# Operands of an output projection made in an earlier stage and kept in DRAM, its last two token tiles by plain products, and GpSimd's sums there on DVE

## Chip, cores, metric

The kernel runs on one core of a Trainium2 chip. The metric is the device time of one launch in microseconds, median over runs. A core has five engines that run their own instruction queues in order: TensorE (PE in the profile, its weight loads PEld), VectorE (DVE), ScalarE (ACT), GpSimd (POOL) and SyncE (SP), which here issues nearly all transfers. SBUF is the memory on the chip, PSUM the accumulators of the matmuls, DRAM the memory off it.

## The reference

One layer of a bidirectional encoder for two sequences, 1024 and 256 tokens of width D = 1024, together T = 1280 tokens, all in float32.

```
h = rms_norm(x, norm_g) * (1 + scale) + shift
p = h @ w_in                       # gates, the conv branch, q, k, v, o, z
y_conv = cb * conv3(cc * cx) * silu(cz)
y_m    = sigmoid(o) * norm(mlstm both ways(q, k, v, gates)) * silu(mz)
merged = g_conv * (y_conv @ w_proj_conv) + g_mlstm * (y_m @ w_proj_mlstm)
return rms_norm(x + gate * (merged @ w_out), final_norm_g)
```

The change concerns w_out (1024 x 1024, the output projection) and the last two lines.

## The kernel before, in words

Float32 accuracy is had from faster matmuls: each operand is split into a high part (a cast on ACT, "wh" or "H") and a low part (source minus high part, "wl" or "L"), and each matmul becomes three: high x high, high x low, low x high. Large products are done by Strassen's scheme: a 2 x 2 block product takes seven products of sums of blocks, where the plain way takes eight of the blocks themselves.

The work stands in this order.

1. The main stage, the input projection (L809). One product is 24 matmuls of 128 x 320: 4 slices k, 3 part pairs, 2 token groups. For each, `prep` loads raw weights (512 KB a pair), DVE makes a sum where the scheme asks for one (L674), ACT casts (L319) and POOL subtracts (L320). Each wh and each wl lies in one of four slots of a ring; a slot comes free when the last instruction that reads it is done. The first 77 products are the gate part with the first head's products; then `gate_inputs` runs, and `advance(n)` emits products up to number n.
2. The mLSTM stage, with further matmuls woven in (L1403 to L1652).
3. The merging stage (`merge`, L1855 to L1857): 16 blocks, each of two products of 24 matmuls of 128 x 320, one for each branch and token half. Results of two units share a PSUM tile of two banks; DVE reads each (L619) and multiplies it by a gate. Loads named th and zc bring gates and earlier results from DRAM. In blocks 4, 6, 9 and 11, `prepare(k)` makes a quarter of the operands of the output projection out of w_out: four loads of 256 KB, sums on DVE (L1800), splits on ACT (L1776) and DVE (L1778), eight stores of 256 KB. Operands b11, b21 and t2 stay in SBUF; t1, t3, t4 and b22 go to DRAM (L1797) and are fetched later.
4. The output stage: tokens in two quads (512 tokens each) and a pair (256). Each takes seven Strassen products (L1947 to L1949) of matmuls 512 columns wide. A product's results go from PSUM through DVE (L1974), get the gate (L1988), are added to x (L1992), squared and summed on ACT (L1997), and normed (L2040, L2036). POOL does a few of these: sums of the next tokens' blocks (L1921), multiplications by the norm's gain (`weigh`, L2122) and, for the pair, one gate and one addition. Of the pair, the very last product is done in two halves of 256 columns, with a short chain behind each (L2230 to L2237), then square root, Newton step and scaling (L2241 to L2266), and the stores of the output.

A class `Board` collects the instructions of a stage with their buffers, and plays them in an order that a cost model finds; each carries a step, and a later step may not go far ahead of an earlier one. The order on each engine is fixed at the build, and a wait holds everything behind it on the same engine.

Of the kernel before, what the change touches and what calls it, by code (L numbers as in the profile page):

```python
# [181 lines left out]
def encoder_kernel(  # L182
# [41 lines left out]
    late_dr = {nm: dram.tile([2, P, 4, 512], F32, name=nm + "_dr") for nm in ("t1", "t3", "t4", "b22")}  # L224
# [1049 lines left out]

    beginning()
    advance(ends[0] - 10)
# [475 lines left out]
    prstack = ctx.enter_context(ExitStack())  # L1752
    pr = prstack.enter_context(tc.tile_pool(name="pr", bufs=7))
# [28 lines left out]
    def prepare(k):  # L1782

        r11, r12, r21, r22 = raws = [buf(pr, [P, 512], F32, "pr", 7) for _ in range(4)]
        for i, raw in enumerate(raws):
            kt, n0 = k + 4 * (i // 2), 512 * (i % 2)
            load(256, lambda raw=raw: raw[:], w_out[0, kt * P:(kt + 1) * P, n0:n0 + 512], (), [raw], True)

        def kept_split(dst, x):
            split_into(lambda: dst[:, 0, k], lambda: dst[:, 1, k], lambda: x[:], [x], (dst, 0, k), (dst, 1, k))  # L1790

        def away(nm, x, spent=True):
            h = buf(pr, [P, 512], F32R, "pr", 7)
            l = x if spent else buf(pr, [P, 512], F32R, "pr", 7)
            split_into(lambda: h[:], lambda: l[:].bitcast(F32R), lambda: x[:], [x], h, l)
            for i, t in enumerate((h, l)):
                op("SP", 256, lambda i=i, t=t: dma(late_dr[nm][i, :, k], fp(t[:])), r=[t], w=[(nm, i, k)], low=True)  # L1797

        def comb(out, x, y, o=ALU.subtract):
            op("DVE", .69, lambda: V.tensor_tensor(out=out[:], in0=x[:], in1=y[:], op=o), r=[x, y], w=[out])  # L1800

        kept_split(B11, r11)
        kept_split(B21, r21)
        away("b22", r22, False)
        comb(r22, r22, r12)
        comb(r12, r12, r11)
        comb(r11, r22, r11, ALU.add)
        away("t1", r12)
        away("t3", r22)
        kept_split(T2, r11)  # L1810
        comb(r21, r21, r11)
        away("t4", r21)
# [65 lines left out]
    class Tokens:  # L1878
# [60 lines left out]
        def product(self, nm, rhs, dst, cs=slice(0, 512)):  # L1939

            for j in range(self.n):
                ap, tok = dst[j]
                wh, wl = self.ws[nm][j]
                for k in range(4):
                    def mm(k=k, ap=ap, wh=wh, wl=wl):
                        m = ap()[:, 0:cs.stop - cs.start]
                        PE.matmul(m, wh[:, k], rhs[:, 0, k, cs], start=k == 0, stop=False)  # L1947
                        PE.matmul(m, wh[:, k], rhs[:, 1, k, cs], start=False, stop=False)  # L1948
                        PE.matmul(m, wl[:, k], rhs[:, 0, k, cs], start=False, stop=k == 3)  # L1949
                    op("PE", .72 * (cs.stop - cs.start) / 512, mm, r=[wh, wl, (rhs, 0, k), (rhs, 1, k)] + ([tok] if k else []), w=[tok])  # L1950
# [127 lines left out]
    prstack.close()  # L2078
# [6 lines left out]
    def fetch(nm):  # L2085
        b = buf(late, [P, 2, 4, 512], F32R, "late", 3)
        for i in range(2):
            for k in (0, 2):
                load(512, lambda i=i, k=k: fp(b[:, i, k:k + 2]), late_dr[nm][i, :, k:k + 2], (), [(b, i, k), (b, i, k + 1)])
        return b  # L2090
# [35 lines left out]
    for st, nxt in ((quad0, quad1), (quad1, pair)):  # L2126
# [15 lines left out]
        if st is quad1:  # L2142
            weigh(0, 0)
# [7 lines left out]
        do(st, "s1", t1, d)  # L2151
        w = st.plus(u3, d, o_tile("o"))
# [7 lines left out]
        if st is quad1:  # L2160
            t3 = fetch("t3")
# [4 lines left out]
        nxt.sums(True)  # L2166
# [7 lines left out]
        if st is quad1:  # L2174
            weigh(0, 1)
# [4 lines left out]
    banks_ = [buf(pool, [P, 2, 512], F32, "acc", 1 if pool is psD else 3) for pool in (psO, psO, psO, psD)]  # L2180
    b, d, c, a, f, e, *gb = [[((lambda t=t, i=i: t[:, i]), (t, i))] for t in banks_ for i in range(2)]

    def out(eng, ap, half, toks, c):
# [3 lines left out]
        else:  # L2187
            op("SP", 256, lambda: dma(q, ap()), r=toks)

    do(st, "a11", B11, b)  # L2190
    s1 = st.copy_out(b, "raw")
    parts(st, "s1", "s2")
    do(st, "s1", t1, d)
    t4 = fetch("t4")
    parts(st, "a12")
    do(st, "s2", T2, c)
    st.rest()
    u2 = st.plus(s1, c, o_tile("o"))
    u4 = st.plus(u2, d, o_tile("raw"))
    st.gated(0, 1, u4, square=False, pool=True)  # L2200
    parts(st, "s3")
    do(st, "a12", B21, a)
    st.plus(s1, a)
    st.gated(0, 0, s1)
    weigh(0, 0)
    parts(st, "s4")
    do(st, "s3", t3, f)
    u3 = st.plus(u2, f, o_tile("raw"))
    w = st.plus(u3, d, o_tile("o"))
    st.gated(1, 1, w)  # L2210
    weigh(1, 1)
    st.gated(1, 0, u3, square=False)
    parts(st, "a22")
    do(st, "s4", b22, e)
    t = o_tile("o")
    st.gated(0, 1, t, e)
    weigh(0, 1)
    ms, q_, t_ = (buf(small, [P, 1], F32, "l" + nm, 1) for nm in "mqt")
    ssq, ssq0 = st.ssq[1], st.ssq[0]
    op("DVE", .1, lambda: V.tensor_scalar(out=ms[:], in0=ssq[:, 0, 1:2], scalar1=1.0 / D, scalar2=EPS, op0=ALU.mult,  # L2220
                                          op1=ALU.add), r=[(ssq, 0, 1)], w=[ms])
    lt = o_tile("raw")
    oap, otoks = st.out_place(1, 0)
    hap, htoks = st.out_place(1, 1)
    gate0 = st.gate(1, 0)
    for i in range(2):
        do(st, "a22", t4, gb[i], cs=slice(256 * i, 256 * i + 256))
# [36 lines left out]
    for half in range(2):  # L2264
        ap, toks = st.out_place(0, half)
        op("ACT", .57, lambda ap=ap: A.activation(ap(), ap(), AF.Copy, bias=0.0, scale=q[:, 0:1]), r=[q, *toks], w=toks)  # L2266
        out("SP", ap, half, toks, 7)
# [30 lines left out]
```

## Time and profile before

| | us |
|---|---|
| median of three runs (1681.29 to 1687.9) | 1683.1 |
| the profiled execution, timed | 1685.18 |
| its span from first to last instruction | 1683.1 |
| merging stage | 1437.3 to 1563.9 |
| quads | 1563.9 to 1644.1 |
| pair, PE's part | 1644.1 to 1668.4 |
| behind the last matmul | 1668.4 to 1683.1 |

Rows of the profile give busy time, count and mean; rows of the timeline give start and length in us, engine, line and operation, and in brackets how long the engine had been idle and what released it.

### The profile page before, as it was taken

Reading aid. Unit: us, or ns where it says so; the run is one execution under the profiler, and the core shown is the slowest. Engines: PE = TensorE matmul, PEld = TensorE weight load, DVE = VectorE, ACT = ScalarE, POOL = GpSimd, SP = SyncE. Lnnn points to the kernel's source line nnn. Section 1 sums busy time; section 2 is a strip of 40 time slices with the busy share of each in tenths; the row PEclk is TensorE's granted clock in tenths of the full one; section 3 lists DMA queues with packets and bytes.
Section 4 is the critical chain, followed back from the end, with each engine's and each line's share of the span. In section 5 each row is a group of like instructions: output and inputs, shape, how many; then the busy total and the mean of one; then the engine's idle time right before and its main releaser. Section 6 shows DMA issues by size and latency. Waiting matters only on the chain.

```text
span 1683.1 us, 27858 instructions
## 1 busy us (share of the span) xinstructions
PE 1626.4 (97%) x10480; PEld 1555.1 (92%) x10480; DVE 1050.0 (62%) x1764; ACT 588.1 (35%) x1145; POOL 678.2 (40%) x492
## 2 busy tenths in 40 slices
PE   6999999999999999999999999999999999989995
PEld 3989999999999999999999999999988898989774
DVE  5785433556555656556666887551267777657798
ACT  4643331135443222222222212212256665423243
POOL 1343333335564666666766533333210002333112
PEclk8999999999999999999999999999999999999998
DMA  9434335324552122222222556459778855888854
GB/s 361 128 100 134 101 105 116 85 64 135 154 153 92 50 73 70 70 82 71 67 60 87 145 130 141 120 124 318 241 244 291 264 159 174 286 301 283 293 176 174
DMA packets 293929, 261.80 MB, mean 156 GB/s; under 512 B 97588, under 2 KB 239140, under 8 KB 293796
## 3 DMA queue, kind: packets, MB, share of 16 engines
q1 hardware_dynamic: 293492, 259.76, 50.2%
q8 instruction: 83, 1.36, 0.3%
q14 instruction: 50, 0.41, 0.1%
q10 hardware_dynamic: 304, 0.27, 0.1%
HBM read 182.70 MB, written 77.28 MB: 154 GB/s over the span
## 4 chain that ended last, share of the span: by engine, by line
PE 86%; DVE 5%; DMA 5%; issue 1%; SPq 1%; ACT 1%; POOL 0%; ACTq 0%; DVEq 0%; POOLq 0%
PE acc L809 64%; PE u L1443 3%; PE qc L1403 3%; PE acc L1650 2%; PE acc L1651 2%; PE acc L1652 2%; PE acc L1947 2%; PE acc L1948 2%; PE acc L1949 2%; DMA th<-th_dr 1%; PE misc L1526 1%; PE misc L1486 1%; SPq L308 1%; DMA raw<-in_w_proj_mlstm_dram 1%; DMA raw<-in_w_in_dram 1%
## 5 line engine op out<-in xcount | busy, mean ns | idle before, releaser
L320 POOL TENSOR_TENSOR wl<-comb,wh 128x512 fp32r<-128x512 f32 x176 | 249.7, 1419 | 288.2 <-ACT wh L319 283.9
L320 POOL TENSOR_TENSOR wl<-raw,wh 128x512 fp32r<-128x512 f32 x168 | 236.4, 1409 | 306.3 <-ACT wh L319 279.9
L718 DVE TENSOR_TENSOR q<-acc,q 128x640 f32<-128x640 f32 x272 | 220.8, 819 | 220.5 <-PE acc L809 215.2
L809 PE MATMUL acc<-xt,wh 128*128 128x320 f32 x1408 | 263.9, 309 | 0.0
L809 PEld LDWEIGHTS acc<-xt,wh 128*128 128x128 f32 x1408 | 220.8, 188 | 0.2
L319 ACT CAST wh<-raw 128x512 fp32r<-128x512 f32 x168 | 103.6, 620 | 323.4 <-PE acc L809 210.4
L319 ACT CAST wh<-comb 128x512 fp32r<-128x512 f32 x176 | 108.8, 619 | 296.2 <-PE acc L809 259.5
L809 PE MATMUL acc<-xt,wl 128*128 128x320 f32 x704 | 160.4, 309 | 0.0
L1609 POOL TENSOR_TENSOR wl<-raw,wh 128x512 fp32r<-128x512 f32 x28 | 36.6, 1310 | 223.3 <-ACT wh L1608 216.2
L809 PEld LDWEIGHTS acc<-xt,wl 128*128 128x128 f32 x704 | 117.7, 188 | 0.0
L674 DVE TENSOR_TENSOR comb<-raw 128x512 f32<-128x512 f32 x88 | 71.6, 814 | 45.1 <-DMA raw<-in_w_in_dram 32.6
L877 POOL TENSOR_TENSOR big<-big,q 128x640 f32<-128x640 f32 x48 | 78.6, 1638 | 37.3 <-DVE q L718 28.9
L616 ACT ACTIVATE q<-q,zero 128x640 f32<-128x640 f32 x76 | 63.1, 831 | 83.7 <-DVE q L718 78.1
L674 DVE TENSOR_TENSOR comb<-raw,comb 128x512 f32<-128x512 f32 x44 | 46.6, 1060 | 62.9 <-POOL wl L320 62.9
L809 PE MATMUL acc<-t3L,wh 128*128 128x320 f32 x352 | 81.5, 313 | 2.7 <-DVE t3L L371 2.7
L809 PE MATMUL acc<-t3H,wh 128*128 128x320 f32 x352 | 81.2, 312 | 1.4 <-ACT t3H L370 1.4
L809 PE MATMUL acc<-b00H,wh 128*128 128x320 f32 x352 | 82.4, 316 | 0.0
L809 PE MATMUL acc<-b10H,wh 128*128 128x320 f32 x352 | 80.7, 310 | 0.8 <-ACT q L732 0.8
L809 PE MATMUL acc<-t3H,wl 128*128 128x320 f32 x352 | 81.3, 312 | 0.0
L809 PE MATMUL acc<-b11H,wh 128*128 128x320 f32 x352 | 81.1, 312 | 0.0
L809 PE MATMUL acc<-b00L,wh 128*128 128x320 f32 x352 | 80.8, 311 | 0.0
L809 PE MATMUL acc<-t2L,wh 128*128 128x320 f32 x352 | 80.4, 310 | 0.1
(400 smaller groups left out, 4096.5 us busy)
## 6 DMA issues: line engine op xcount, KB each, us to landing
raw<-in_w_in_dram SPq DMA_DIRECT2D x120, 256.0 KB
raw<-in_w_in_dram SPq DMA_DIRECT2D x34, 512.0 KB
late<-t_dr SPq DMA_DIRECT2D x24, 512.0 KB
th<-th_dr SPq DMA_DIRECT2D x31, 320.0 KB
th_dr<-q SPq DMA_DIRECT2D x28, 320.0 KB
raw<-in_w_proj_conv_dram SPq DMA_DIRECT2D x16, 512.0 KB
raw<-in_w_proj_mlstm_dram SPq DMA_DIRECT2D x16, 512.0 KB
k<-kn_dr SPq DMA_DIRECT2D x56, 128.0 KB
```

The costliest lines, as they stand in the source:

```text
L319: op("ACT", .63, lambda: A.copy(wh[:], src()), r=r, w=[wh])
L320: op("POOL", 1.4, lambda: G.tensor_tensor(out=wl[:], in0=src(), in1=fp(wh[:]), op=ALU.subtract), r=[*r, wh], w=[wl])
L616: A.activation(out, in_, AF.Tanh, bias=zero[:, 0:1], scale=0.5)
L674: op("DVE", .9, lambda: V.tensor_tensor(out=t[:], in0=x(), in1=y(), op=o), r=[x.tok, y.tok], w=[t])
L718: op("DVE", .82, lambda: V.tensor_tensor(out=two(dst()), in0=acc[:, :, 0:TQ], in1=two(t()), op=ALU.add), r=[acc, t.tok], w=[dst.tok])
L809: PE.matmul(acc[:, q, 0:TQ], st_[:, k_, :], m_[:, q * TQ:(q + 1) * TQ], start=k_ == 0 and n == 0, stop=k_ == 3 and n == 2)
L877: op("POOL", 1.65, lambda: G.tensor_tensor(out=dst(), in0=dst(), in1=t(), op=ALU.mult), r=[dst.tok, t.tok], w=[dst.tok])
L1403: PE.matmul(pq[:, 0:HD + 2], qTs[i][:, kd, c * P:(c + 1) * P], C[:, kd, :], start=kd == 0, stop=kd == 1)
L1443: PE.matmul(pu[:, db, 0:HD + 2], k[:, db * P:(db + 1) * P], wv[:], start=True, stop=True)
L1609: op("POOL", 1.36, lambda wh=wh, wl=wl, src=src: G.tensor_tensor(out=wl[:], in0=src(), in1=fp(wh[:]), op=ALU.subtract), r=[raw, wh], w=[wl])
L1650: PE.matmul(acc[:, :TQ], wh, yH, start=kt == 0, stop=False)
L1651: PE.matmul(acc[:, :TQ], wh, yL, start=False, stop=False)
```

## The change

There are four edits.

The splits of w_out move from the merging stage to the main stage. A generator `out_weights` runs beside the products 31 to 70: for each of four k it loads four blocks of 256 KB, and then, one operand with each product, makes eight operands: cast on ACT (L1293), subtraction on POOL (L1294), in wh and wl slots of the same ring of four, and two stores of 256 KB (L1297) to DRAM; four sums go to DVE (L1300). That is 32 casts, 32 subtractions, 64 stores, 16 sums and 16 loads. The merging stage now only fetches b11, b21 and t2, 12 loads of 512 KB.

The generator yields 40 times, so that product 70 is emitted in its loop; `advance(ends[0] - 7)` then sets the counter back to 70, and `advance(ends[0])` emits product 70 again: 24 more matmuls of 128 x 320, one more POOL subtraction and two more raw loads of 512 KB.

The pair is done by plain products: eight in place of seven, of the four blocks of tokens without sums, each pair of products summed in PSUM; the last two of them are done in halves of 256 columns (48 matmuls in place of 24). Operand b12 is fetched for it, t3 and t4 only for the quads.

On POOL, the sums of the second quad go to DVE, the pair's sums and the pair's gate and addition are gone, and so are four multiplications of the second quad, which are now in DVE's scaling. Two multiplications stay on POOL for the pair, and one half of the last tile is scaled on DVE in place of ACT.

```diff
+    def out_weights():
+        for k in range(4):
+            places = [big() for _ in range(2)]
...
+            for _ in range(1 + 4 * (k == 0)):
+                yield
+            def parts(nm, x):
+                wh, wl = (buf(wp, [P, 4, P], F32R, t, 4) for t in ("wh", "wl"))
...
+                op("ACT", .63, lambda: A.copy(flat(wh), x[0]()), r=[x[1]], w=[wh])
+                op("POOL", 1.4, lambda: G.tensor_tensor(out=flat(wl), in0=x[0](), in1=fp(flat(wh)), op=ALU.subtract),
+                   r=[x[1], wh], w=[wl])
+                for i, t in enumerate((wh, wl)):
+                    op("SP", 256, lambda i=i, t=t, k=k: dma(op_dr[nm][i, :, k], fp(flat(t))), r=[t], low=True)
...
+            yield parts("b22", r22)
+            yield parts("b12", r12)
+            comb(r22, r22, r12)
+            yield parts("t3", r22)
...
     beginning()
-    advance(ends[0] - 10)
+    advance(31)
+    for _ in out_weights():
+        advance(at[0] + 1)
+    advance(ends[0] - 7)
     board.step = at[0]
     gate_inputs()
     advance(ends[0])
...
-        if i in (4, 6, 9, 11):
-            prepare((4, 6, 9, 11).index(i))
+        if i in (5, 7, 9):
+            n_ = (5, 7, 9).index(i)
+            fetch_into((B11, B21, T2)[n_], ("b11", "b21", "t2")[n_], low=True)
...
-        nxt.sums(True)
+        if nxt is quad1:
+            nxt.sums()
...
+    left, right = ("a11", "a12"), ("a21", "a22")
+    parts(st, "a12", "a21", "a22")
+    both_halves(0, left, (B11, B21), p0)
+    st.gated(0, 0, o_tile("raw"), p0)
     weigh(0, 0)
...
     for i in range(2):
-        do(st, "a22", t4, gb[i], cs=slice(256 * i, 256 * i + 256))
+        both_halves(1, right, (b12, b22), gb[i], cs=slice(256 * i, 256 * i + 256))
```

What this does to the order shows on POOL in the gate part of the main stage. Before, ahead of the first head's products, POOL's queue is one subtraction for each product (L320; comb and raw are sums and raw weights):

```order
L320 TENSOR_TENSOR wl_2485<-comb_2265,wh_2476 128x512 [waits DVE_49,PE_49,Activation_49]
L320 TENSOR_TENSOR wl_2519<-comb_2300,wh_2511 128x512 [waits DVE_49,PE_49,Activation_49]
L320 TENSOR_TENSOR wl_2560<-comb_2232,wh_2552 128x512 [waits PE_49,Activation_49]
L320 TENSOR_TENSOR wl_2587<-raw_2196,wh_2577 128x512 [waits PE_49,Activation_49]
L320 TENSOR_TENSOR wl_2626<-comb_2333,wh_2615 128x512 [waits DVE_49,PE_49,Activation_49]
```

At the end of the same part now, w_out's subtractions (L1294, from big) alternate with those of the products (L320):

```order
L320 TENSOR_TENSOR wl_2944<-raw_2631,wh_2924 128x512 [waits PE_49,Activation_49]
L1294 TENSOR_TENSOR wl_2960<-big_2811,wh_2947 128x512 [waits PE_49,Activation_49,Pool_49]
L320 TENSOR_TENSOR wl_3007<-comb_2717,wh_2996 128x512 [waits PE_49,Activation_49,Pool_49]
L1294 TENSOR_TENSOR wl_3016<-big_2691,wh_2999 128x512 [waits DMAHW2_49,DMAHW0_49,Activation_49]
L320 TENSOR_TENSOR wl_3037<-comb_2760,wh_3027 128x512 [waits PE_49,Activation_49]
L1294 TENSOR_TENSOR wl_3051<-big_2811,wh_3039 128x512 [waits PE_49,Activation_49]
L320 TENSOR_TENSOR wl_3074<-comb_2674,wh_3059 128x512 [waits DMAHW0_49,Activation_49]
L1294 TENSOR_TENSOR wl_3092<-big_2691,wh_3071 128x512 [waits DMAHW3_49,PE_49,Activation_49]
L320 TENSOR_TENSOR wl_3120<-raw_2631,wh_3108 128x512 [waits DMAHW0_49,Activation_49]
L1294 TENSOR_TENSOR wl_3132<-big_2691,wh_3112 128x512 [waits DMAHW2_49,Activation_49]
L320 TENSOR_TENSOR wl_3153<-comb_2796,wh_3124 128x512 [waits PE_49,Activation_49]
L1294 TENSOR_TENSOR wl_3173<-big_2691,wh_3151 128x512 [waits PE_49,Activation_49]
```

Ahead of each of a product's subtractions there now stands one of w_out's, and both wait for PE or for a store where their slot was last used. In the addresses that the build gives, the slots before go round strictly in four; now wl_2944, wl_3007, wl_3037 and wl_3051 lie in one and the same slot, one after the other, and wl_3120, wl_3153 and wl_3173 in another.

SP's queue in the merging stage before has stores of the operands (L1797) among the loads that the stage itself needs (zc, th):

```order
L1797 DMA b22_dr_80<-pr_15654 128x512 [waits DMAHW2_49,Activation_49]
L1797 DMA b22_dr_80<-pr_15664 128x512 [waits DMAHW3_49,DVE_49]
L1797 DMA t1_dr_77<-pr_15694 128x512 [waits DMAHW4_49,Activation_49]
L1797 DMA t1_dr_77<-pr_15560 128x512 [waits DMAHW5_49,DVE_49]
L1797 DMA t3_dr_78<-pr_15716 128x512 [waits DMAHW6_49,Activation_49]
L308 DMA zc_15736<-zc_dr_64 128x640 [waits DMAHW7_49,DVE_49]
L308 DMA th_15738<-th_dr_72 128x640 [waits DMAHW0_49]
```

Now the same queue, some blocks into the stage, has whole loads of made operands (t2) in their place, with waits on transfers only:

```order
L308 DMA t2_15764<-t2_dr_79 128x1024
L308 DMA t2_15764<-t2_dr_79 128x1024 [waits DMAHW3_49]
L308 DMA zc_15784<-zc_dr_64 128x640 [waits DMAHW4_49,DVE_49]
L308 DMA th_15793<-th_dr_72 128x640 [waits DMAHW6_49,DMAHW5_49]
L308 DMA zc_15814<-zc_dr_64 128x640 [waits DVE_49]
L308 DMA th_15817<-th_dr_72 128x640 [waits DMAHW7_49]
```

The loads of the stage thus no longer stand behind stores that wait for casts and subtractions.

More of the change, by code (lines that the diff above doesn't have):

```diff
@@ L1780, in split_into, with fetch_into @@
             op("POOL", 1.4, lambda: G.tensor_tensor(out=lo(), in0=src(), in1=fp(hi()), op=ALU.subtract), r=[*r, wh], w=[wl])
[L1782 to L1812, printed above, removed]
+    def fetch_into(b, nm, ks=(0, 2), low=False):
+        for i in range(2):
+            for k in ks:
+                load(512, lambda i=i, k=k: fp(b[:, i, k:k + 2]), op_dr[nm][i, :, k:k + 2], (), [(b, i, k), (b, i, k + 1)], low)
     def second_ym(n):
@@ L1937, in rest, with product @@
             self.comb(self.places[0, 1], self.places[0, 1], self.places[0, 0])
[L1939 removed]
+        def product(self, nm, rhs, dst, cs=slice(0, 512), start=True, stop=True):
             for j in range(self.n):
@@ L2086, in fetch @@
         b = buf(late, [P, 2, 4, 512], F32R, "late", 3)
-        for i in range(2):
-            for k in (0, 2):
-                load(512, lambda i=i, k=k: fp(b[:, i, k:k + 2]), late_dr[nm][i, :, k:k + 2], (), [(b, i, k), (b, i, k + 1)])
+        fetch_into(b, nm)
         return b
@@ L2188, in out, with both_halves @@
             op("SP", 256, lambda: dma(q, ap()), r=toks)
[L2190 to L2204, printed above, removed]
-    weigh(0, 0)
[L2206 to L2217, printed above, removed]
+    def both_halves(r, lhs, rhs, dst, **kw):
+        for i in range(2):
+            do(st, lhs[i], rhs[i], dst, start=i == 0, stop=i == 1, **kw)
+    left, right = ("a11", "a12"), ("a21", "a22")
+    parts(st, "a12", "a21", "a22")
+    both_halves(0, left, (B11, B21), p0)
+    st.gated(0, 0, o_tile("raw"), p0)
+    weigh(0, 0)
+    both_halves(1, right, (B11, B21), p1)
+    st.gated(1, 0, o_tile("raw"), p1)
+    weigh(1, 0)
+    both_halves(0, left, (b12, b22), p2)
+    st.gated(0, 1, o_tile("raw"), p2)
     ms, q_, t_ = (buf(small, [P, 1], F32, "l" + nm, 1) for nm in "mqt")
     ssq, ssq0 = st.ssq[1], st.ssq[0]
-    op("DVE", .1, lambda: V.tensor_scalar(out=ms[:], in0=ssq[:, 0, 1:2], scalar1=1.0 / D, scalar2=EPS, op0=ALU.mult,
-                                          op1=ALU.add), r=[(ssq, 0, 1)], w=[ms])
+    op("DVE", .1, lambda: V.tensor_scalar(out=ms[:], in0=ssq[:, 0, 0:1], scalar1=1.0 / D, scalar2=EPS, op0=ALU.mult,
+                                          op1=ALU.add), r=[(ssq, 0, 0)], w=[ms])
     lt = o_tile("raw")
-    oap, otoks = st.out_place(1, 0)
-    hap, htoks = st.out_place(1, 1)
-    gate0 = st.gate(1, 0)
+    oap, otoks = st.out_place(1, 1)
+    hap, htoks = st.out_place(1, 0)
+    gate0 = st.gate(1, 1)
     for i in range(2):
-        do(st, "a22", t4, gb[i], cs=slice(256 * i, 256 * i + 256))
+        both_halves(1, right, (b12, b22), gb[i], cs=slice(256 * i, 256 * i + 256))
         board.step = step[0] - 2
@@ L2265, in encoder_kernel @@
         ap, toks = st.out_place(0, half)
-        op("ACT", .57, lambda ap=ap: A.activation(ap(), ap(), AF.Copy, bias=0.0, scale=q[:, 0:1]), r=[q, *toks], w=toks)
+        if half == 0:
+            op("ACT", .57, lambda ap=ap: A.activation(ap(), ap(), AF.Copy, bias=0.0, scale=q[:, 0:1]), r=[q, *toks], w=toks)
+        else:
+            op("DVE", .69, lambda ap=ap: V.scalar_tensor_tensor(
+                out=ap(), in0=ap(), scalar=q[:, 0:1], in1=fng[:, 512:1024].rearrange("p (g c) -> p g c", g=2), op0=ALU.mult,
+                op1=ALU.mult), r=[q, fng, *toks], w=toks)
         out("SP", ap, half, toks, 7)
```

54 lines of the change are left out of this document (32 added, 22 removed).

## The prediction

> **What bounds the kernel now.** I read the busy shares on the page first, then the waits of PE, then each stage by windows, and last the timeline at the places that the change touches.
>
> ```profile
> PE 1626.4 (97%) x10480; PEld 1555.1 (92%) x10480; DVE 1050.0 (62%) x1764; ACT 588.1 (35%) x1145; POOL 678.2 (40%) x492
> ```
>
> PE is busy for 97% of the span, so what counts is where PE stands idle, and how many matmuls it gets. The stages of the change, in windows (width, then busy time of PE, PEld, DVE, ACT, POOL, granted clock, DMA share, GB/s):
>
> ```profile
> 126.00:296.00 170.00, 169.13 (x1154) 167.24 (x1153) 71.84 (x90) 50.12 (x73) 59.69 (x46) 1.00 0.40 113
> 1437.30:1563.90 126.60, 117.70 (x771) 115.33 (x770) 84.78 (x122) 42.75 (x71) 43.60 (x30) 0.97 0.86 286
> 1563.90:1644.10 80.20, 78.85 (x337) 62.81 (x337) 69.37 (x84) 28.84 (x58) 12.86 (x6) 1.00 0.73 248
> 1644.10:1668.40 24.30, 20.59 (x97) 16.06 (x95) 23.18 (x38) 10.57 (x23) 8.42 (x6) 1.00 0.61 220
> 1668.40:1683.10 14.70, 0.01 (x1) 0.00 (x0) 8.82 (x25) 3.42 (x7) 2.23 (x2) 0.63 0.22 72
> ```
>
> The gate part is full, the merging stage loses 9 us, the pair 4, and behind the last matmul stand 14.7 us without PE. The waits of PE, first of the gate part, then of the merging stage, then of the output stage:
>
> ```profile
> PE acc L988 <- ACT big L999: 0.9, 1, 0.9
> ...
> PE acc L1855 <- DVE th L619: 8.9, 9, 3.5
> ...
> PE acc L1947 <- DVE raw L1974: 2.3, 1, 2.3
> PE acc L1947 <- ACT raw L1961: 2.0, 3, 0.7
> PE acc L1947 <- DVE o L1974: 0.8, 1, 0.8
> ```
>
> So there is time to be had in the merging stage and at the end, and none in the gate part, where the work is put.
>
> **The gate part: what is added.** One product there:
>
> ```profile
> 161.97 0.62 ACT L319 CAST wh<-comb 128x512 fp32r<-128x512 f32 x1 [1.59 <-PE acc L809]
> 162.01 0.46 PE L809 MATMUL acc<-b11H,wh 128*128 128x320 f32 x2
> 162.60 0.46 PE L809 MATMUL acc<-b11H,wl 128*128 128x320 f32 x2
> 162.67 1.30 POOL L320 TENSOR_TENSOR wl<-comb,wh 128x512 fp32r<-128x512 f32 x1 [2.22 <-ACT wh L319]
> 163.93 0.32 SPq L311 DMA_DIRECT2D th_dr<-q  x1
> 165.54 0.46 PE L809 MATMUL acc<-t2H,wh 128*128 128x320 f32 x2
> ```
>
> From 162.01 to 165.54 a product takes 3.53 us, .147 for each of 24 matmuls. It needs its high part at once and its low part .59 later. The product emitted twice costs 3.5 us with certainty: PE has no idle time to take it.
>
> The engines have room. POOL gets 32 more subtractions of 1.30, 41.6 beside 59.7 of 170; ACT 32 casts of .62, 20 beside 50; SP 80 issues of .32. The DMA traffic, 80 times 256 KB or 21 MB in some 160 us, is 130 GB/s on top of 113, under the 286 that the merging stage shows. DVE's sums are 16 of about .7.
>
> What has no room is the ring of slots. In the trace the cast starts when a product's end frees its slot, and a whole product lies between. Where the slot of the next split is that of the product just ending, nothing lies between, and PE stands. There are three forms in the order, for the last six products of this part. If only POOL waits (wl_3007), the low part is 1.30 and about .3 of handing over late, less .59: 1.0 us. If cast and subtraction wait (wl_3037, wl_3153), it is .62 + 1.30 + .1 − .59 = 1.4. If w_out's split stands ahead on both engines (wl_3051 before wl_3074, wl_3092 before wl_3120, wl_3173 before wl_3195), it is .62 + 1.30 + 1.30 + .1 − .59 = 2.7. The sum is 1.0 + 2 × 1.4 + 3 × 2.7 = 11.9, of which .9 takes the place of the wait at L988 that is there already: 11.0. With the repeated product the gate part costs 14.5. For the other 26 splits I take nothing: their slots were last used a product earlier, and POOL's two subtractions, 2.6, fit into 3.53.
>
> The bounds of this term: 3.5 if each of these waits is hidden by a lead that the splits keep; 14.5 + 10.6 if the other splits starve too, which is a rival below. I stay at 14.5, since the slots are fixed by the build.
>
> **The merging stage: what is taken away.** Its one long stall, and a short one:
>
> ```profile
> 1478.94 0.88 DVE L619 SCALAR_TENSOR_TENSOR th<-th,acc 128x320 f32<-128x320 f32 x2 [1.36 <-DMA th<-th_dr]
> 1481.16 0.89 DVE L1863 TENSOR_TENSOR mg<-th,zc 128x320 f32<-128x320 f32 x2 [1.34 <-DMA zc<-zc_dr]
> 1482.52 0.64 PE L1855 MATMUL acc<-y,wh 128*128 128x320 f32 x1 [3.54 <-DVE th L619]
> ...
> 1488.13 0.31 PE L1855 MATMUL acc<-y,wh 128*128 128x320 f32 x1
> ...
> 1490.20 0.31 PE L1857 MATMUL acc<-y,wl 128*128 128x320 f32 x1
> 1491.09 0.41 PE L1855 MATMUL acc<-y,wh 128*128 128x320 f32 x1 [0.58 <-DVE th L619]
> ```
>
> ```profile
> 1482.00:1486.00 4.00, 3.48 (x13) 3.48 (x14) 2.40 (x5) 1.52 (x3) 0.99 (x1) 0.50 1.03 390
> ```
>
> DVE was late because th and zc were: their loads stand in SP's queue behind w_out's, on DMA engines that are full. Behind the 3.54 the clock fell to .50, and 21 matmuls from 1482.52 to 1488.13 took 5.6 us in place of 3.1. With half of the traffic gone (12 loads of 512 KB against 16 loads and 32 stores of 256 KB), both go, 3.5 + 2.5.
>
> The .58 stays: the second unit of a two-bank PSUM tile waits until DVE has read the first, .89 from start to start in place of .147, so .74 each. By the order there are ten such pairs now, nine before. The stage then is 32 products of 3.53, 113.0, and 10 × .74: 120.4 against 126.6, **−6.2**. The ends: −3.5 if only the stall goes and a smaller one takes over, −9 if the short waits go as well.
>
> **Quads and pair.** The pair has 72 matmuls of 512 columns as before and 24 more of 256:
>
> ```profile
> 1660.57 0.40 PE L1949 MATMUL acc<-late,wl 128*128 128x512 f32 x1
> 1663.22 0.50 PE L1947 MATMUL acc<-late,wh 128*128 128x512 f32 x1 [2.25 <-DVE raw L1974]
> 1663.56 0.40 PE L1948 MATMUL acc<-late,wh 128*128 128x512 f32 x1
> 1663.79 0.39 PE L1949 MATMUL acc<-late,wl 128*128 128x512 f32 x1
> ...
> 1665.42 0.28 PE L1947 MATMUL acc<-late,wh 128*128 128x256 f32 x1
> 1665.54 0.28 PE L1948 MATMUL acc<-late,wh 128*128 128x256 f32 x1
> ```
>
> At .23 and .12 from start to start that is +2.8. The waits for scheme results go, the 2.25 among them; two waits on shared PSUM tiles come, near the .74 and, the half tile at the end, near 1.2. So 72 × .233 + 48 × .118 + 2.0 = 24.5 against 24.3: +.2. In the quads DVE takes over two sums of 1.22 (a 128x1024 operation, below) and four scalings of .7, 5 us in a stage where it has 11 free, but not evenly:
>
> ```profile
> 1594.00:1636.00 42.00, 41.33 (x178) 32.93 (x177) 40.95 (x56) 16.38 (x35) 7.42 (x4) 1.00 0.58 187
> 1646.07 1.22 DVE L1988 TENSOR_TENSOR o<-o,y 128x1024 f32<-128x1024 f32 x1
> ```
>
> I take +.5, with 0 and +5 as ends.
>
> **Behind the last matmul.** These rows decide it:
>
> ```profile
> 1665.13 0.68 DVE L1988 TENSOR_TENSOR o<-o,y 128x512 f32<-128x512 f32 x1
> 1666.20 3.17 POOL L2122 TENSOR_TENSOR y<-y,fng 128x512 f32<-128x512 f32 x2 [6.98 <-ACT raw L1997]
> 1666.46 1.79 DVE L1988 TENSOR_TENSOR raw<-raw,y 128x512 f32<-128x512 f32 x1
> ...
> 1672.68 0.42 DVE L2230 TENSOR_TENSOR raw<-acc,y 128x256 f32<-128x256 f32 x1
> 1673.60 1.39 DVE L2234 CUSTOM_DVE_ANT_0 raw<-y 128x256 f32<-128x256 f32 x1
> 1676.38 0.75 DVE L2249 SCALAR_TENSOR_TENSOR y<-y,lq,fng 128x512 f32<-128x512 f32 x1
> 1677.88 1.33 ACT L2266 ACTIVATE y<-y,q 128x512 f32<-128x512 f32 x2 [0.71 <-DVE q L2244]
> ```
>
> The last matmul ends at 1668.4, but DVE comes to its result only at 1672.68: it still has two tiles of scheme results to finish, and was slowed by POOL, 1.79 for what takes .68 alone. From 1672.68 to 1677.13 the chain takes 4.45, of which .97 is such a slowing (1.39 for an operation that takes .42 in the first half). From the last scaling's end, 1679.21, to the end of the span, 1683.1, a store takes 3.9. After the change DVE has nothing left over, so the end is 3.5 of chain and 3.9 of store: 7.4 in place of 14.7, **−7.3**. The ends: −4 if the scaling of the second tile still comes last, −8.
>
> That POOL and DVE shut each other out is what the Trainium skill, "SBUF — State Buffer", section "Who interferes with whom", states: an operation of DVE with two inputs in SBUF and one of GpSimd that reads SBUF exclude each other for a whole instruction. The trace agrees (1.79 against .68). The rule speaks against putting subtractions on POOL beside new sums on DVE: by it the four sums that fall among the last six products could hold POOL in the gaps by 4 × .68 = 2.7, and the sum below would be +4.4. I leave this out, because each of these sums overwrites a block that POOL's subtraction reads, and so follows it.
>
> **The sum.** 14.5 − 6.2 + .2 + .5 − 7.3 = +1.7 us. The span becomes 1684.8. The profiled execution timed 2.1 above its span and above the median, so the median too goes from 1683.1 to **1684.8**: no change that can be told, since half a per cent (8.4 us) is about what a measurement of this kernel can tell from none.
>
> **Rivals.**
> *The ring copes.* The splits keep a lead and the six waits vanish; all that is added is the repeated product. For it speaks that POOL and ACT are free for more than half of the time; against it, that the slots are the build's. 1684.8 − 11 = 1673.8, faster.
> *The ring starves everywhere.* A slot used by w_out's split is free only when its store has been read out. Two products are 7.06; cast and subtraction of both kinds take 3.84, so a store of over 3.2 us decides. The load of zc, issued at 1477.61, was waited for until 1481.16, 3.55, on engines over 90% busy:
>
> ```profile
> 1477.61 0.32 SPq L308 DMA_DIRECT2D zc<-zc_dr  x1
> ```
>
> At that price each of 32 products loses .33, 10.6 in all: 1695.4, slower. Against it: the DMA engines are at .40 here.
> *The clock falls in the gaps of 2.7.* The trace has 3.54 with a fall and 2.25 without; each fall cost 2.5, three would give +7.5, 1692.3. The Trainium skill, "TensorE: Matmul & The Clock Gate", section "HAM oscillation — how this bites in real kernels", allows gaps up to about 3.4 us; by it none falls and the sum stands. The 3.54 and the 2.25 both agree.
> *DVE becomes the bound in the quads*, at its 40.95 of 42: +5 in place of +.5, 1689.3.
> *It does not do what it says*: the product that is made twice is this case, and is in the sum.
>
> **How the numbers follow.** The forecast, within half a per cent, .61; the ring copes .20; it starves .11; the clock falls .04; DVE bound .04. Faster is .20, same .61 + .04 = .65, slower .11 + .04 = .15. The range goes from the first rival, 1673.0, to the second, 1696.0.
>
> **What would show it.** Right: in the gate part PE waits for POOL's wl at L809, three times near 2.7 and three between 1.0 and 1.4, at the clock 1.00; 24 more matmuls there; no wait over 1.5 at L1869 in the merging stage, and its 120 us; under 8 us behind the last matmul. Wrong: waits of PE spread over all of the gate part, or none; DVE's waits for th in the merging stage as long as now, since the fetches take the place of the stores; a last chain that still ends on a second tile.

## The result, and the profile after

The changed kernel takes 1698.84 us (median of five runs, 1697.61 to 1700.25) against 1685.72 of the kernel before (five runs, 1681.29 to 1688.9): a ratio of 1.008, interval 1.006 to 1.0101. It is slower, by 13 us, where no change that can be told was forecast, and lies above the forecast's range. The profiled execution took 1700.25, with a span of 1698.5.

Where the 15.4 us between the two spans are, by the starts of the first and last matmul of each stage in the two timelines:

| us | before | after | moved | forecast |
|---|---|---|---|---|
| start of the first product (L809) | 30.4 | 29.1 | −1.3 | 0 |
| main stage, first to last product | 1126.7 | 1150.2 | +23.5 | +14.5 |
| mLSTM stage | 280.2 | 284.7 | +4.5 | 0 |
| merging stage | 126.5 | 121.7 | −4.8 | −6.2 |
| output stage to the last matmul | 104.3 | 104.9 | +.6 | +.7 |
| from the last matmul's start | 15.0 | 7.9 | −7.1 | −7.3 |

So the two lower rows came as forecast, and the loss is in the main stage and a little in the mLSTM stage. The windows of the changed kernel: three of the gate part, then merging stage, quads, pair, and behind the last matmul (columns as before):

```profile
126.00:226.00 100.00, 100.00 (x684) 100.00 (x683) 57.67 (x60) 38.79 (x60) 56.15 (x40) 1.00 0.60 198
226.00:290.00 64.00, 58.94 (x392) 57.16 (x391) 35.10 (x37) 21.82 (x36) 40.77 (x30) 1.00 0.81 243
290.00:323.00 33.00, 24.05 (x128) 21.43 (x128) 13.99 (x18) 5.70 (x10) 13.90 (x10) 0.90 0.70 179
1464.00:1585.70 121.70, 115.50 (x771) 112.86 (x770) 45.74 (x78) 26.68 (x43) 41.48 (x30) 1.00 0.71 245
1585.70:1666.10 80.40, 79.05 (x339) 62.99 (x338) 63.88 (x85) 28.78 (x59) 0.00 (x0) 1.00 0.74 262
1666.10:1690.90 24.80, 22.95 (x121) 18.93 (x119) 20.85 (x45) 7.40 (x19) 2.59 (x2) 1.00 0.25 85
1690.90:1698.50 7.60, 0.01 (x1) 0.00 (x0) 2.89 (x10) 1.01 (x2) 0.00 (x0) 0.78 0.41 138
```

The first 100 us of the gate part are full, though w_out's splits run beside them from 174 on. From 226 on PE stands 5 of 64 us, and then 9 of 33, there at a clock of .90. Its waits in the whole gate part:

```profile
PE acc L809 <- POOL wl L320: 8.8, 10, 1.7
PE acc L809 <- ACT wh L319: 5.2, 6, 1.4
```

The forecast had 11.9 us in six places; there are 14.0 in sixteen waits, 9.9 of them in eleven waits at the last six products and 4.1 in five waits at four products before. One product of the last six, in the timeline:

```profile
296.03 0.46 PE L809 MATMUL acc<-t3H,wl 128*128 128x320 f32 x2
296.27 0.62 ACT L1293 CAST wh<-big 128x512 fp32r<-128x512 f32 x1 [4.39 <-PE acc L809]
296.80 0.61 ACT L319 CAST wh<-comb 128x512 fp32r<-128x512 f32 x1
296.97 1.28 POOL L1294 TENSOR_TENSOR wl<-big,wh 128x512 fp32r<-128x512 f32 x1 [3.73 <-ACT wh L1293]
297.46 0.85 PE L809 MATMUL acc<-xt,wh 128*128 128x320 f32 x4 [0.98 <-ACT wh L319]
298.21 1.26 POOL L320 TENSOR_TENSOR wl<-comb,wh 128x512 fp32r<-128x512 f32 x1
299.52 0.90 PE L809 MATMUL acc<-xt,wl 128*128 128x320 f32 x2 [1.20 <-POOL wl L320]
300.22 1.27 PE L809 MATMUL acc<-xt,wh 128*128 128x320 f32 x4
```

This is the third form of the forecast, row by row: ACT waits for the product that ends at 296.3, casts for w_out first, then for the product; POOL does the same; and PE stands twice, .98 for the high part and 1.20 for the low one. What was not forecast stands in the last row: four matmuls take 1.27, since the clock has fallen: it was .75 on the mean from 297 to 301.

The places before the last six had no wait in the forecast. Two of them in the timeline, the first with the store that ends it:

```profile
225.88 0.47 SPq L1297 DMA_DIRECT2D b_dr<-wh  x1
232.71 0.62 ACT L319 CAST wh<-comb 128x512 fp32r<-128x512 f32 x1 [3.70 <-DMA b_dr<-wh]
233.38 0.56 PE L809 MATMUL acc<-t2H,wh 128*128 128x320 f32 x2 [1.35 <-ACT wh L319]
...
276.78 0.62 ACT L1293 CAST wh<-big 128x512 fp32r<-128x512 f32 x1 [8.41 <-DMA big<-in_w_out_dram]
280.05 0.56 PE L809 MATMUL acc<-b00H,wl 128*128 128x320 f32 x2 [0.90 <-POOL wl L320]
```

At 233 the product's cast stands 3.70 until a store of w_out's part, issued 6.8 before, gives its slot back. At 280 ACT stands 8.41 for a load of w_out, with the products' casts queued behind it. The waits at 250 and 261 are behind stores too, issued at 244.33 and 254.45 and waited for until 248.0 and 259.8.

At the end, in the timeline, DVE comes to the last half .2 after PE, and nothing of GpSimd is in its way:

```profile
1690.94 0.42 DVE L2225 TENSOR_TENSOR raw<-acc,y 128x256 f32<-128x256 f32 x1 [0.19 <-PE acc L1963]
1691.40 0.42 DVE L2227 TENSOR_TENSOR y<-y,raw 128x256 f32<-128x256 f32 x1
1691.86 0.43 DVE L2229 CUSTOM_DVE_ANT_0 raw<-y 128x256 f32<-128x256 f32 x1
...
1694.49 0.46 ACTq L2195 DMA_DIRECT2D out_dram<-y  x1
```

From there to the end of the span a store takes 4.0.

### The profile page after: what moved, and what is told of

The parts are those of the page before. It is cut to its first block, busy times and chain, and to the rows that moved or that the text cites. A ratio compares the mean times of both kernels' runs of the same rounds, so it can differ in the third digit from the quotient of the medians.

```text
span 1698.5 us, 28022 instructions
## 1 busy us (share of the span) xinstructions
PE 1640.0 (97%) x10528; PEld 1564.9 (92%) x10528; DVE 1031.7 (61%) x1731; ACT 584.8 (34%) x1142; POOL 704.7 (41%) x514
## 4 chain that ended last, share of the span: by engine, by line
PE 75%; DMA 2%; DVE 2%; ACT 1%; SPq 0%; issue 0%; POOL 0%; ACTq 0%; DVEq 0%
PE acc L809 50%; PE u L1486 3%; PE qc L1446 3%; PE acc L1961 2%; PE acc L1962 2%; PE acc L1963 2%; PE acc L1694 2%; PE acc L1693 2%; PE acc L1869 2%; PE acc L1695 2%; PE acc L1870 2%; PE acc L1871 2%; DMA th<-th_dr 1%; PE misc L1569 1%; PE misc L1529 1%; PE acc L988 1%
## 5 line engine op out<-in xcount | busy, mean ns | idle before, releaser
L320 POOL TENSOR_TENSOR wl<-comb,wh 128x512 fp32r<-128x512 f32 x176 | 251.5, 1430 | 257.7 <-ACT wh L319 236.3
L320 POOL TENSOR_TENSOR wl<-raw,wh 128x512 fp32r<-128x512 f32 x169 | 237.8, 1408 | 274.7 <-ACT wh L319 258.9
L809 PE MATMUL acc<-xt,wh 128*128 128x320 f32 x1408 | 264.8, 310 | 2.0 <-ACT wh L319 2.0
L809 PEld LDWEIGHTS acc<-xt,wh 128*128 128x128 f32 x1408 | 221.7, 188 | 2.6 <-ACT wh L319 2.5
L809 PE MATMUL acc<-xt,wl 128*128 128x320 f32 x704 | 161.2, 310 | 2.4 <-POOL wl L320 2.4
L809 PEld LDWEIGHTS acc<-xt,wl 128*128 128x128 f32 x704 | 118.1, 188 | 2.9 <-POOL wl L320 2.9
L674 DVE TENSOR_TENSOR comb<-raw 128x512 f32<-128x512 f32 x88 | 79.6, 905 | 59.3 <-DMA raw<-in_w_in_dram 34.6
L619 DVE SCALAR_TENSOR_TENSOR th<-th,acc 128x320 f32<-128x320 f32 x62 | 29.9, 485 | 94.0 <-PE acc L1871 42.9
L809 PE MATMUL acc<-b00H,wh 128*128 128x320 f32 x360 | 85.0, 318 | 1.0 <-ACT wh L319 1.0
L809 PE MATMUL acc<-b00H,wl 128*128 128x320 f32 x360 | 83.1, 312 | 2.6 <-POOL wl L320 2.6
L809 PE MATMUL acc<-t3L,wh 128*128 128x320 f32 x352 | 81.4, 313 | 2.7 <-DVE t3L L371 2.7
L809 PE MATMUL acc<-b00L,wh 128*128 128x320 f32 x360 | 83.2, 313 | 0.0
L809 PE MATMUL acc<-t3H,wh 128*128 128x320 f32 x352 | 81.4, 313 | 1.7 <-ACT t3H L370 1.2
L809 PE MATMUL acc<-t2H,wl 128*128 128x320 f32 x352 | 80.5, 310 | 1.8 <-POOL wl L320 1.8
L809 PE MATMUL acc<-b11H,wl 128*128 128x320 f32 x352 | 80.3, 309 | 1.5 <-POOL wl L320 1.5
L809 PE MATMUL acc<-b11H,wh 128*128 128x320 f32 x352 | 81.3, 312 | 0.5 <-ACT wh L319 0.5
```

Source lines behind the costliest of these rows:

```text
L320: op("POOL", 1.4, lambda: G.tensor_tensor(out=wl[:], in0=src(), in1=fp(wh[:]), op=ALU.subtract), r=[*r, wh], w=[wl])
L674: op("DVE", .9, lambda: V.tensor_tensor(out=t[:], in0=x(), in1=y(), op=o), r=[x.tok, y.tok], w=[t])
L809: PE.matmul(acc[:, q, 0:TQ], st_[:, k_, :], m_[:, q * TQ:(q + 1) * TQ], start=k_ == 0 and n == 0, stop=k_ == 3 and n == 2)
```

## The experiments

The theories. *Ring*: w_out's splits and the products' own share four slots, and the build has placed some of them so that a split waits for the product just ending. *Traffic*: 80 more transfers make stores and loads late, and so everything that waits for them. *GpSimd*: two subtractions in a row are what is waited for. The first part of a run is the main stage of the table above; in the kernel before it is 1126.7, and 3.5 more with the product that is made twice, 1130.2. Each run was compared with the kernel before on its own chip, whose medians were 1684.5 to 1685.4.

**few_stores**: 48 of the 64 stores left out.

```diff
+                if nm in ("b22", "b12"):
                     for i, t in enumerate((wh, wl)):
                         op("SP", 256, ... dma(op_dr[nm][i, :, k], fp(flat(t))), r=[t], low=True)
```

> The changed kernel that stores only operands b22 and b12 of the eight (16 stores of 64) and fetches them in place of the others, so its output is not the reference's. Stores theory (a slot is held until its store has been read, on transfer queues that are busy): the gaps in the gate part fall from 14 us idle to under 4, and the kernel to about 1684. Slots theory (a slot is held by the product that is just ending): gaps stay at 10 or more, the kernel above 1693.

Measured 1681.06, ratio .9962 (.9948 to .9976). The first part is 1130.2: nothing is left but the product made twice.

```profile
226.00:290.00 64.00, 64.00 (x439) 64.00 (x438) 37.99 (x38) 25.55 (x43) 46.24 (x35) 1.00 0.61 173
```

PE is full where it stood 5 us, with all casts and subtractions in place. GpSimd is busier than in the changed kernel (46.2 against 40.8) and holds nobody up: that theory falls as the main cause. But the stores do two things, they hold slots and they make traffic, so two more kernels try to part these.

**short_stores**: the same order and the same slots, 48 stores cut to 2 partitions, so that they move little and soon give their slots back.

```diff
+                n = P if nm in ("b22", "b12") else 2
-                    op("SP", 256, ... dma(op_dr[nm][i, :, k], fp(flat(t))), r=[t], low=True)
+                    op("SP", 256, ... dma(op_dr[nm][i, 0:n, k], fp(flat(t))[0:n]), r=[t], low=True)
```

> The changed kernel in its own order, 48 of the 64 stores cut from 128 to 2 partitions (the fetches read b22 and b12 in their place, so the output is not the reference's). Ring theory, slots fixed at the build: a split whose slot the product just ending has read still waits for it, whatever the stores take; the gaps at the last six products stay (8 us idle or more of 14), the first part 1142 or more; only the four gaps before them go. Traffic theory: nearly all gaps go, the first part under 1135.

Measured 1695.89, ratio 1.0066 (1.0048 to 1.0085). First part 1141.0, 10.8 above 1130.2. Its waits:

```profile
283.49 0.56 PE L809 MATMUL acc<-t2H,wl 128*128 128x320 f32 x2 [0.92 <-POOL wl L320]
287.15 0.56 PE L809 MATMUL acc<-t3H,wh 128*128 128x320 f32 x2 [0.47 <-ACT wh L319]
288.50 0.56 PE L809 MATMUL acc<-t3H,wl 128*128 128x320 f32 x2 [0.51 <-POOL wl L320]
292.68 0.85 PE L809 MATMUL acc<-xt,wh 128*128 128x320 f32 x4 [0.98 <-ACT wh L319]
294.74 0.56 PE L809 MATMUL acc<-xt,wl 128*128 128x320 f32 x2 [1.21 <-POOL wl L320]
...
310.20 0.56 PE L809 MATMUL acc<-b00H,wh 128*128 128x320 f32 x2 [0.98 <-ACT wh L319]
312.71 0.56 PE L809 MATMUL acc<-b00H,wl 128*128 128x320 f32 x2 [1.66 <-POOL wl L320]
```

```profile
285.00:318.00 33.00, 24.02 (x148) 20.82 (x147) 14.35 (x17) 7.42 (x13) 15.53 (x12) 1.00 0.44 89
```

These are the waits of the changed kernel's last six products, to a hundredth in most rows, with half of its bytes per second (89 GB/s against 179). No transfer makes them: the slots as placed at the build do. What is gone are the waits ahead of 283, and the falls of the clock in this part. The ring theory holds for 10.8 us (1141.0 where its expectation said 1142 or more).

**other_source**: all 64 stores, 48 of them reading a constant tile.

```diff
+                    if nm in ("b22", "b12"): ... (as before)
+                    else:
+                        op("SP", 256, ... dma(op_dr[nm][i, :, k]..., ident[:].unsqueeze(1).to_broadcast([P, 4, P])),
+                           r=(), after=(made_by[i],), low=True)
```

> All 64 stores of the changed kernel are issued, with their bytes, but 48 of them (all operands but b22 and b12) read a constant tile and not the split's slots, so that the output is not the reference's. Ring theory (a store holds one of the four slots until it is done, and that is what the products' splits lack): as without these stores, the first part within 3 us of 1130 and the kernel 1679 to 1686. Traffic theory (80 more transfers on SP's queue and the transfer engines make the products' own loads and stores late): the gaps come back, the first part 1140 or more, the kernel above 1690.

Measured 1689.01, ratio 1.0018 (1.0004 to 1.0033): between the two. First part 1136.5, 6.3 above 1130.2, and one wait with the fall of the clock behind it makes most of it:

```profile
PE acc L988 <- DVE q L718: 4.1, 1, 4.1
```

The sum that stands ahead of it on DVE, and the windows there:

```profile
307.99 0.69 DVE L674 TENSOR_TENSOR comb<-raw 128x512 f32<-128x512 f32 x1 [7.50 <-DMA raw<-in_w_in_dram]
```

```profile
305.00:310.00 5.00, 0.87 (x7) 0.50 (x6) 1.98 (x3) 0.62 (x1) 1.03 (x1) 1.00 1.03 286
310.00:315.00 5.00, 5.00 (x26) 3.40 (x25) 4.06 (x6) 2.00 (x3) 1.53 (x2) 0.66 1.09 210
```

With these slots free, PE waits once for DVE, which itself stands 7.50 for a load of a product's own weights, with the transfer engines at 1.03 at the end of it, and then PE runs at .66; some 2.5 more were lost at three products before. So traffic has a price of its own. Its size need not be that of the real stores: the constant tile is read in rows of 512 bytes, and whether that is dearer was not tried.

**dve_sub**: w_out's subtractions on DVE.

```diff
-                op("POOL", 1.4, lambda: G.tensor_tensor(out=flat(wl), ...
+                op("DVE", .69, lambda: V.tensor_tensor(out=flat(wl), ...
```

> The changed kernel with w_out's subtractions on DVE in place of GpSimd. GpSimd theory (two subtractions in a row on GpSimd, 2.6 us, are what the product's low part waits for): the waits of PE for POOL at L809, 8.8 us, fall under 4 and the kernel to 1692 or less. Slots theory: the waits for the low part shrink by .7 at the three to four places where a w_out split stands ahead, the waits for the high part (5.2) stay: 1695 to 1698. Stores theory: no change, 1698.

Measured 1692.75, ratio 1.0041 (1.0026 to 1.0056): 6 under the changed kernel, between the theories' numbers. The waits for POOL fell from 8.8 to 4.7, those for ACT from 5.2 to 4.1; the first part is 1143.6. The three smaller waits at 250, 261 and 280 are gone, and the long low part (1.20) is .5. The wait at 233 is there as before (1.23 and .56), and the clock falls twice here too: .66 on the mean from 235 to 240 and .57 from 304 to 308. GpSimd's queue makes the ring's waits longer; the high parts still wait .98.

**once**: no product twice.

```diff
-    advance(ends[0] - 7)
+    advance(max(at[0], ends[0] - 7))
```

> The changed kernel with product 70 made once. Slots theory (w_out's splits and the products' splits share a ring of four, so a split waits for the product just ending): only the repeated product goes, 3.5 us, and the gaps stay; 1698.8 - 3.5 = 1695, with 0 to -3 more if the last gap (2.6 idle and a fall of the clock) goes with it. Rival (the repeated product is hidden in time that PE stands anyway): no change, 1698.8.

Measured 1705.58 (1702.1 to 1709.12), ratio 1.0119 (1.0097 to 1.0141): slower than with the product made twice, against both expectations. The four runs are two pairs, near 1702 and near 1709; the profile is of a run of 1702.1, and what the slower pair loses besides is not known. In the gate part the 3.5 are gone and some 2 more. But the order of the products behind it, which is found anew, now has waits that the changed kernel doesn't have, between 430 and 495:

```profile
PE acc L809 <- DVE q L718: 5.4, 3, 2.9
```

These, with a fall of the clock behind the last, cost some 7 us. There POOL stands 4.8 for a DMA with masks' operands and has the products' subtraction behind it:

```profile
482.80 1.29 POOL L1245 TENSOR_TENSOR big<-big,masks 128x512 f32<-128x512 f32 x1 [4.76 <-DMA big<-a_dr]
484.05 1.30 POOL L320 TENSOR_TENSOR wl<-comb,wh 128x512 fp32r<-128x512 f32 x1
```

Taking away work does not take away its time where a planner orders all that follows. Why the planner chose so there was not tried.

**act_queue**: the 64 stores from ACT's queue.

```diff
-                    op("SP", 256, lambda i=i, t=t, k=k: dma(op_dr[nm][i, :, k], fp(flat(t))), r=[t], low=True)
+                    op("ACT", .45, lambda i=i, t=t, k=k: A.dma_start(op_dr[nm][i, :, k], fp(flat(t))), r=[t], low=True)
```

> The changed kernel with w_out's 64 stores issued from ACT's queue in place of SP's. If the four gaps ahead of the last six products come from stores and loads waiting behind each other in SP's queue: they go, the first part 1141 to 1146, the kernel about 1690. If they come from the transfer engines' load: they stay, and ACT, which now waits for GpSimd's subtraction ahead of each store, holds the products' casts: first part 1150 or more, the kernel 1700 or more.

Measured 1692.79, ratio 1.0053 (1.0031 to 1.0076), first part 1144.6. Its waits are others: six for POOL's low part, 5.8 together, and one of 7.6 for DVE (L975) ahead of gate_inputs. Neither expectation tells this apart: the planner counts a slot as free when ACT has issued the store, and so places the slots otherwise. Inconclusive on SP's queue. Late transfers are there all the same: one of the six, 1.31 at 234, is behind a store of ACT's queue that was issued at 226.7 and waited for until 232.5, and DVE had stood 13.3 for a load of a product's weights ahead of the 7.6.

**dve_early**: subtractions on DVE, three products earlier, none twice.

```diff
-    advance(31)
+    advance(28)
-    advance(ends[0] - 7)
+    advance(max(at[0], ends[0] - 10))
```

> The changed kernel with w_out's subtractions on DVE, all of it three products earlier (28 to 67), and no product made twice. If what the subtractions on DVE gave (-6.1) and the repeated product (-3.5) add up and the last three splits leave the first head's products: 1698.8 - 6.1 - 3.5 - 3 = 1686. If it only shifts the same gaps and the order behind them: 1692 or more.

Measured 1690.17, ratio 1.0025 (1.0011 to 1.0038). First part 1139.6. Only six waits, 8.7, are left, but one of 5.3 for ACT is new, at 175: there ACT stands 5.89 for w_out's first load and has the product's cast queued behind it. The clock falls behind it and once more at 303.5. The parts do not add up.

**pair_only**: the pair and GpSimd's part of the change alone; the operands, b12 among them, made in the merging stage.

```diff
+        away("b12", r12, False)
         comb(r22, r22, r12)
```

> The pair by plain products and GpSimd's sums as in the change, but the operands made in the merging stage as before (b12 besides: 4 casts, 4 subtractions and 8 stores more). If the parts are independent, the gate part's +22.9 and the merging stage's -4.8 go, the end's -7.1 and the pair's +.7 stay: 1685.7 - 6.4 = 1679, with up to +3 for b12's work beside full transfers in the merging stage. Rival (the end was short only because DVE came to it less burdened from the merging stage): the end keeps 10 us or more, and the kernel 1682 or more.

Measured 1680.15, ratio .9968 (.9956 to .9979): faster than before, as expected within 1.2. First part 1126.3, merging stage 127.7, output stage 104.9 and 7.7 behind the last matmul's start. The end is short whatever the merging stage does; the rival falls.

**half_move**: besides that, two of the four k in the gate part, at about half the rate.

```diff
-        for k in range(4):
+        for k in range(2):
...
+    advance(31)
+    for _ in out_weights():
+        advance(at[0] + 2 - at[0] % 5 // 3)
+    advance(max(at[0], ends[0] - 10))
```

> The pair by plain products; of the operands only two of four k are made in the gate part, at about half the rate (products 31 to 67, none made twice), the other two in the merging stage as before. Ring theory: with two products for a split the slots suffice, the first part stays within 3 us of before; the merging stage gains 2 to 3 of the 4.8: 1680.2 - 2 = 1678, ratio to before about .995. Traffic theory: half of the gaps stay, +6: 1686 or more.

Measured 1679.82, ratio .9968 (.9955 to .9981). The gate part is full:

```profile
230.00:290.00 60.00, 60.00 (x411) 59.65 (x411) 30.78 (x38) 19.22 (x31) 30.42 (x24) 1.00 0.65 178
290.00:312.00 22.00, 22.00 (x156) 19.68 (x155) 11.74 (x23) 3.54 (x6) 7.17 (x6) 1.00 0.38 79
```

At half the rate the ring and the transfers suffice (first part 1124.8), and the traffic theory's half of the gaps does not come. But the whole is no faster than pair_only: its merging stage is 125.4, and the mLSTM stage, which it does not touch, came out at 284.2.

**before_again** and **after_again**: the two kernels unchanged, for a second profile.

> The kernel before once more, for a second profile. Chance theory: mLSTM stage anywhere from 280 to 285, merging stage from 121 to 128, first part within 1 us of 1126.7, the end 15. Rival: 280.2 and 126.5 again within .5.

> The changed kernel once more, for a second profile. Chance theory for the mLSTM stage (its +4.5 comes from the granted clock and from one late load, not from the change): the stage differs by over 1 us from the first profile's 284.7, and the gap of 1.77 there does not bring the clock down again. Rival (the change delays that stage): 284 to 285 again, with the same fall of the clock. The gaps of the first part are the same in number and size under both.

| us | main | mLSTM | merging | time |
|---|---|---|---|---|
| before, first and second | 1126.7, 1126.3 | 280.2, 283.1 | 126.5, 126.6 | 1685.18, 1687.99 |
| after, first and second | 1150.2, 1148.3 | 284.7, 283.5 | 121.7, 125.7 | 1700.25, 1701.15 |

The main stage comes again within 2 us, with the same waits at the last six products. Against the expectation the waits before them are not the same: that at 233 is 2.06 in place of 1.35 and has a fall of the clock behind it, that at 250 is gone, and so is the fall at 319.5. The mLSTM stage does not come again, by 2.9 in the kernel before, and the two second profiles are .4 apart in it: most of the +4.5 is chance. A part may not be: the wait of PE for th at its start was 2.4 to 2.6 in the six profiles with no product made twice and 2.7 to 4.0 in the seven with it (3.8 and 4.0 in the changed kernel). Why is open. The merging stage gains 4.8 in one profile and .9 in the other.

## Why the prediction was wrong

**The repeated product, +3.5**, is there: without stores the first part is 1130.2, just 3.5 above before.

**The slots, +11.0**, are there too, and of that size: 10.8 in short_stores. They hold product by product. By the starts of the low parts' matmuls in short_stores and few_stores, the last six products lose 1.1, 1.5, 2.7, 2.7, 1.5 and 3.1, where the forecast had 1.0, 1.4, 2.7, 2.7, 1.4 and 2.7; few_stores stands 1.5 ahead of the last one by itself, where the forecast took off .9. Only the sign that was to show it was wrong: PE does not wait 2.7 at once for the low part, but part of it already for the high part (.98 and 1.21), and no single wait for POOL there is over 1.66.

**The step that failed is "For the other 26 splits I take nothing".** The rest of the first part's +23.5, 9.2, is what the whole stores add to short_stores. Four places ahead of the last six products, at 233, 250, 261 and 280, cost 5.7 us by the starts of their products. They are the price of late transfers: they went in short_stores, and the timeline has a store that was late at three of them and a load of w_out at the fourth. "Last used a product earlier" counted the product that reads a slot and left out the store that reads it; the three stores were waited for until 3.7 to 6.8 us after their issue, over the 3.2 that the forecast itself named as the limit. Nearly 3 more are two falls of the clock, at the products of 297.5 (4.03 lost, 2.72 in short_stores) and of 316.3 (12.93 against 11.38, gate_inputs in both). Under 1 us of the 9.2 I cannot place. In the second profile three of the four places cost 6.3, a fall of the clock behind the first of them included, and the fall at 297 is there again, so both terms come again, but not their sizes. The forecast had weighed both as rivals, at .11 and .04: stores over 3.2 us, and a clock that falls in the gaps. It argued against the first that the transfer engines were at .40. That was the share of the kernel before; in the changed kernel it was .81 from 226 to 290, with the new traffic, and just where the first head's products store their q, k and v as well. The 130 + 113 GB/s of the forecast was a mean over the part, and the measured 243 is that sum; the error was to hold it against the highest rate seen in the profile, 286, as if all below that were free. At 173 GB/s and .61 (few_stores) PE was full in the same stretch. Whether the stores were late for the load on the engines or for their place in SP's queue, no run parts cleanly.

**The clock rival** was priced at single gaps of 2.7 against 3.54 and 2.25. It fell instead after two shorter ones, .98 and 1.20, with four matmuls between. The Trainium skill, "TensorE: Matmul & The Clock Gate", section "HAM oscillation — how this bites in real kernels", which the forecast drew on, allows gaps up to about 3.4 us; by it the clock would not have fallen, and the measurement decides. What counted was not the length of one gap (see the last section).

**The merging stage, −6.2**: −4.8 and −.9. The stall of 3.54 and its fall of the clock are gone in the first profile, ten short waits stand as counted (6.2 us together, none over 1.0), but in the second one of 2.2 takes over. The lower end that the forecast gave, "−3.5 if only the stall goes and a smaller one takes over", was still too hopeful there.

```profile
PE acc L1869 <- DVE th L619: 6.2, 10, 1.0
...
PE acc L1869 <- DVE th L619: 8.5, 11, 2.2
```

(The first row is of the first profile of the changed kernel, the second of its second.)

**Quads and pair, +.7, and the end, −7.3**, were right: +.6 and −7.1. That the first agrees so well is luck in part: by the windows the quads took +.2 and the pair +.5, where the forecast had +.5 and +.2. The end is the forecast's chain and store, 3.6 and 4.0 for 3.5 and 3.9. In the quads DVE took over GpSimd's sums at no loss, 63.9 us busy of 80.4.

**The mLSTM stage** was taken as unmoved; +4.5 in the first two profiles and +.4 in the second two, most of it chance.

So the change is two changes. One, the pair and the end, is worth 5 us (pair_only, 1680.15 against 1685.35 on its chip). The other, moving the operands, buys 1 to 5 in the merging stage and costs 22 to 23.5 in the main stage, 3.5 of it for the product that is made twice; with half of the operands, at half the rate and no product twice, it costs nothing and buys about as little.

## What to carry to other kernels

Work moved under a full engine is paid in what it borrows, slots and transfers, not in engine time: count for how long each buffer is held, from the cast to the landed store, against how many there are, and set the new traffic against the share of the stretch that it goes into with its own traffic added. Then spread it until a whole product lies between a slot's last reader and its next writer; here half the rate was enough. And test the parts of a bundled change apart: here one of them alone was faster than either kernel.

## What the runs showed of the hardware

The same gap does not always bring the clock down. In the mLSTM stage PE stands 1.77 us at one place in both profiles of each of the two kernels; in three of the four the clock stays at 1.00, and in the first profile of the changed kernel it falls. The windows around it, of the first profiles of before and of after:

```profile
1419.00:1423.00 4.00, 2.23 (x14) 1.85 (x13) 3.19 (x14) 1.83 (x6) 0.46 (x1) 1.00 0.90 295
1423.00:1427.00 4.00, 4.00 (x30) 3.94 (x29) 2.79 (x7) 2.44 (x7) 0.00 (x0) 1.00 0.19 65
```

```profile
1444.00:1448.00 4.00, 2.23 (x8) 1.83 (x9) 3.14 (x13) 1.75 (x6) 0.78 (x1) 0.74 0.87 274
1448.00:1452.00 4.00, 4.00 (x25) 3.81 (x25) 1.89 (x6) 1.78 (x6) 0.00 (x0) 0.83 0.14 55
```

Busy times are the same in both, 2.23 and 4.00. What differs is where the gap lies on the clock's own time. In each trace every stretch of half clock starts on a grid of 3.41 us. The pair of gaps .98 and 1.2 brought the clock down in the changed kernel and not in short_stores; cut on the grid, the changed kernel (first two rows) has .98 and a good half of the second gap in one stretch, and short_stores (last two) has one gap in each:

```profile
295.62:299.03 3.41, 1.72 (x10) 1.19 (x9) 0.82 (x1) 1.14 (x2) 2.06 (x2) 1.00 0.99 275
299.03:302.44 3.41, 2.92 (x11) 2.92 (x12) 0.00 (x0) 0.00 (x0) 0.43 (x1) 0.50 0.84 177
...
290.10:293.51 3.41, 2.43 (x15) 1.93 (x14) 0.82 (x1) 1.14 (x2) 1.33 (x2) 1.00 0.54 82
293.51:296.93 3.42, 2.21 (x16) 2.19 (x16) 0.00 (x0) 0.00 (x0) 1.18 (x1) 1.00 0.21 20
```

Over all thirteen profiles, from 105 us on, each of the 35 stretches at full clock in which PE stood 1.99 us or more was followed by one at .50, and none in which it stood under 1.48; in between, 8 of 24 were. The 2.25 us gap that the forecast took for harmless lies across a border of the grid, 1.05 on one side and 1.21 on the other, and of the 3.54 one stretch has 2.12.

The Trainium skill, "TensorE: Matmul & The Clock Gate", section "What's actually happening", says that the activity window is 3413 ns long, runs freely and doesn't start with the kernel. The traces agree: within each one the falls start whole multiples of 3.41 us apart. By a table in the same section of the Trainium skill the clock falls after an idle window of about 3.4 us; here 1.48 of 3.41 was enough at one place and 1.99 everywhere. A fall costs 1.3 to 2.5 us here, so a kernel with several gaps near 2 us has a spread of a few us that no edit explains.
